# Weight sums of the second MLP product: formed by VectorE beside the product, or by accumulating DMAs in DRAM during the scan

## The chip, the cores and the metric

The kernel runs on one core of a Trainium2 chip. The metric is device time in microseconds for one execution of the whole program, taken as the median of several executions. Beside it stands one profiled execution, whose trace gives every instruction on TensorE (PE, with its weight loads as PEld), VectorE (DVE), ScalarE (ACT), GpSimd (POOL) and SyncE (SP), and every DMA. The clock that TensorE was granted in that execution was 0.999 of full speed.

## The reference

One decoder layer over 16 meta tokens and 512 tokens of width 1024. The front half projects the normed input, mixes tokens by causal pooling and by a Mamba-2 scan in chunks of 128 tokens (8 groups of 4 heads), gates the two branches and multiplies by `w_o`. The back half is a squared-ReLU MLP:

```python
v = rmsnorm(h, mlp_norm_w[i])
hid = jax.nn.relu(v @ w_ff1[i])
h = h + (hid * hid) @ w_ff2[i]      # 512x4096 by 4096x1024
out = rmsnorm(h, final_norm_w)[:, N_META:]
```

All is float32. What the change touches is the last product, `(hid * hid) @ w_ff2`.

## The kernel before, in words

**Precision and operands.** Every large product is made of three TensorE passes on a high and a low part of each operand. A weight block of 128x1024 (512 KB) is loaded by SyncE, its high part is a ScalarE copy and its low part a VectorE subtraction of the high part from the block. In the front half this is `block()` (lines 78 to 93): three tiles for the raw block (`raw`), four pairs for the parts (`whi`, `wlo`). In the back half the same is done by `split` (lines 924 to 930).

**The scan.** Lines 706 to 714 run over eight groups, g = 0 to 7. Each turn weaves the steps of `ssd(g)` (line 448), the scan of group g, with the steps of a projection for the next group, so that TensorE always has matmuls between the scan's small ones. `ssd(g)` begins with one DMA from GpSimd's queue (line 456): it broadcasts the cumulated decays of the group from DRAM to a 1 MB tile `abc`. There is one such tile, so the load waits until the matmuls `py` of the group before (line 543) have read it. ScalarE then makes `eb` from it (line 491), ScalarE and VectorE turn it into the decay matrix (lines 494 to 503), VectorE masks it (line 530), and the `py` matmuls read it (line 543). The instructions of each engine are issued in one fixed order.

In groups 1, 2, 3 and 5 (`SUMS_AT`) the weave has a third member, `sums_of_u` (line 682): it loads two blocks of the projected input from DRAM by GpSimd's queue, forms sums of them on VectorE, and stores high and low parts into the DRAM tiles `t_d` (lines 702 and 703). After the scan, 16 GpSimd DMAs load these again (lines 831 to 833) for the pooling products, which begin with `pool_pair` (line 758). Later, GpSimd's queue loads the residual `ht` (line 964). Nothing else uses GpSimd's queue; it is served in order.

**The MLP.** The hidden width of 4096 is cut into eight pieces c of 512. For each piece four tiles of the first product (`ff1_tile`, line 1122) give the squared activations. The second product of pieces 0 to 6 is made by a scheme with seven products of half-size blocks in place of eight: activations are cut into two token halves and two hidden halves, the weights of a piece into four quarters of 512 KB called b11, b12, b22 and b21. The scheme needs the activation sums S1 to S4 (made in `ff1_tile`) and four weight sums:

- t1 = b11 + b12
- t2 = t1 + b22
- s3 = b12 + b22
- t4 = t2 + b21

In the kernel before, `quarter` (line 1115) loads the four quarters by SyncE into a pool of six tiles, and `sum_of` (line 1175) makes the four sums on VectorE, three of them in place. The loop is at lines 1213 to 1240. Each of the seven operands (b11, t2, s3, t4, b22, b21, t1) is split, and its `prod` (line 1157) is 12 matmuls with 512 columns. Between the products stand `ff1_tile` calls (`filler`). Piece 7 is done without the scheme (lines 1244 to 1276), and each token tile is normed and stored as it is finished. On the host, `_weight_blocks` packs all weights into one input `w`, in the order in which SyncE loads them.

Of the kernel before, what the change touches and what calls it, by code (L numbers as in the profile page):

```python
# [57 lines left out]
def kernel(ctx: ExitStack, tc, xT, x, w, vec, fnw, out):  # L58
    nc = tc.nc
    act, dve, pe, pool = nc.scalar, nc.vector, nc.tensor, nc.gpsimd  # L60

# [620 lines left out]
    def sums_of_u(k, g):  # L682
        a, b = (tsp.tile([P, 2 * TN], F32, tag=t, name=f"{t}{k}") for t in ("ua", "ub"))

        with tc.issue_after(abc_load[g].ins):
            for t, kk in ((a, k), (b, k + 4)):
                nc.gpsimd.dma_start(t, u_d[kk])
        yield
        with tc.issue_after(masked[g].ins):
            dve.tensor_tensor(a[:, one], a[:, two], a[:, one], op=ALU.subtract)  # L690
            dve.tensor_tensor(a[:, two], b[:, two], a[:, two], op=ALU.subtract)
            dve.tensor_tensor(b[:, two], b[:, two], a[:, one], op=ALU.subtract)
            dve.tensor_tensor(b[:, one], b[:, one], b[:, two], op=ALU.subtract)
        yield
        for src, n in ((a, "13"), (b, "42")):
            hi, lo = (tsp.tile([P, 2 * TN], F32R, tag=f"t{p}", name=f"t{p}{n}{k}") for p in "hl")
            if n == "42":
                yield
            with tc.issue_after((y_first if n == "13" else squared)[g].ins):
                act.copy(hi, src)  # L700
            dve.tensor_tensor(lo, src, hi.bitcast(F32), op=ALU.subtract)
            nc.gpsimd.dma_start(t_d[n, "h", k], hi)
            nc.gpsimd.dma_start(t_d[n, "l", k], lo)
# [220 lines left out]
    def split(src):  # L924
        hi = wp.tile([P, 1024], F32R, tag="whi", name=f"shi{nsplit[0]}")
        lo = wp.tile([P, 1024], F32R, tag="wlo", name=f"slo{nsplit[0]}")
        nsplit[0] += 1
        act.copy(hi, src)  # L928
        dve.tensor_tensor(lo, src, hi.bitcast(F32), op=ALU.subtract)  # L929
        return hi, lo  # L930
# [181 lines left out]
    NC = 8  # L1112
    rel = {}

    def quarter(tag):
        b = nblk[0]
        nblk[0] += 1
        t = qp.tile([P, 1024], F32, tag="quarter", name=f"{tag}{b}")
        nc.sync.dma_start(t, w[b])
        return t  # L1120

    def ff1_tile(c, f):
# [49 lines left out]
    p2v = [p2[:, :512], p2[:, 512:]]  # L1172
    q5v = [psum1(f"q5_{t}") for t in range(2)]

    def sum_of(a, b, name, out=None):
        t = out if out is not None else qp.tile([P, 1024], F32, tag="quarter", name=name)
        dve.tensor_tensor(t, a, b, op=ADD)
        return t

    def squares(t, c, n):  # L1180
        act.activation(junk[:, : c.stop - c.start], ht[:, t, c], AF.Square, accum_out=fs[:, t, n : n + 1])

# [28 lines left out]
            ff1_tile(*order.pop(0))  # L1211

    for c in range(NC - 1):
        b11, b12, b22, b21 = (quarter(n) for n in ("b11_", "b12_", "b22_", "b21_"))
        z, e = c == 0, c == NC - 2
        prod(av, c, A11, split(b11), True, False)
        onto(0, 0, alpha, ADD)
        t1 = sum_of(b11, b12, "", b11)
        t2 = sum_of(t1, b22, f"t2_{c}")
        filler()  # L1220
        prod(av, c, S2, split(t2), False, False)
        onto(0, 1, alpha, SUB)
        filler()
        prod(av, c, S3, split(sum_of(b12, b22, "", b12)), False, False)
        onto(1, 1, alpha, SUB)
        filler()
        prod(av, c, A22, split(sum_of(t2, b21, "", t2)), False, True)
        onto(1, 0, alpha, ADD)
        if e:
            prod(q5v, c, S1, split(t1), z, True)  # L1230
# [5 lines left out]
        prod(av, c, S4, split(b22), True, True)  # L1236
        onto(0, 1, alpha, ADD)
        prod(p2v, c, A12, split(b21), z, False)
        if not e:
            prod(q5v, c, S1, split(t1), z, False)  # L1240
    assert not order


# [1 line left out]
    hh, hl = rel[c]  # L1245
    wq = {}
    for k, half in ((1, 0), (1, 1), (0, 1), (0, 0)):
        wq[k, half] = split(quarter(f"w{k}{half}_"))
    lastp = psum2("last")
    for t in range(4):  # L1250
        T, st = t // 2, slice((t % 2) * P, (t % 2 + 1) * P)
# [28 lines left out]
def _weight_blocks(i):  # L1280

    w_in, w_g, w_up = i["w_in"][0], i["pool_w_group"][0], i["w_pool_up"][0]
    w_so, w_o, f1, f2 = i["w_ssd_out"][0], i["w_o"][0], i["w_ff1"][0], i["w_ff2"][0]
    blocks = []

    def cols(m, c):
        a = m[:, c : c + P]
        return a.reshape(NK, P, P).transpose(1, 0, 2).reshape(P, NK * P)

    def put(b):  # L1290
        blocks.append(b)
# [68 lines left out]
    def quarters(c):  # L1360
        for k, half in ((1, 0), (1, 1), (0, 1), (0, 0)):
            put(quarter(c, k, half))
# [9 lines left out]
    for c in range(8):  # L1372
        quarters(c)
        for _ in range(3 if c > 4 else 4):
            ff1()
    return np.ascontiguousarray(np.stack(blocks))


def _vectors(i):
# [35 lines left out]
```

## Time and profile before

| | |
|---|---|
| Time, median of 3 | 1012.66 us (1012.47 to 1012.91) |
| The profiled execution's own time | 1013.65 us |
| Its span, first to last instruction | 1012.0 us |
| DMA traffic | 118.41 MB, mean 117 GB/s |
| GpSimd's DMA queue (q0) | 23.86 MB, 6.8% of the time of 16 DMA engines |
| SyncE's DMA queue (q1) | 92.75 MB, 28.3% |

The profile gives, for each engine, busy time and its share of the span. A view by stretches of time gives the same for each stretch, with the mean busy share of the 16 DMA engines and the bytes per second. The timeline lists instructions in order: start, duration, engine, line, operation, operands, and in square brackets how long the engine stood idle before it and what ended that. The list of DMA issues gives the size of each and the median time from its issue to the landing of its last byte. The time that lies outside the span, 1013.65 - 1012.0 = 1.65 us, has no instruction.

### The profile page before, as it was taken

Reading aid. Unit: us, or ns where it says so; the run is one execution under the profiler, and the core shown is the slowest. Engines: PE = TensorE matmul, PEld = TensorE weight load, DVE = VectorE, ACT = ScalarE, POOL = GpSimd, SP = SyncE. Lnnn points to the kernel's source line nnn. Section 1 sums busy time; section 2 is a strip of 40 time slices with the busy share of each in tenths; the row PEclk is TensorE's granted clock in tenths of the full one; section 3 lists DMA queues with packets and bytes.
Section 4 is the critical chain, followed back from the end, with each engine's and each line's share of the span. In section 5 each row is a group of like instructions: output and inputs, shape, how many; then the busy total and the mean of one; then the engine's idle time right before and its main releaser. Section 6 shows DMA issues by size and latency. Waiting matters only on the chain.

```text
span 1012.0 us, 14216 instructions
## 1 busy us (share of the span) xinstructions
PE 1002.7 (99%) x5661; PEld 866.4 (86%) x5661; DVE 763.4 (75%) x1039; ACT 561.9 (56%) x748; POOL 35.8 (4%) x72
## 2 busy tenths in 40 slices
PE   9999999999999999999999999999999999999997
PEld 7889899998889998978898888888888888888886
DVE  7988798978736587888789557887676686676866
ACT  8665958595827439473355333466545455354444
POOL 0010000101000000003000001000000000000000
PEclk9999999999999999999999999999999999999999
DMA  7263243616224231418334534033333324323112
GB/s 245 84 237 114 67 137 115 204 50 201 66 91 147 101 126 43 146 39 258 102 104 162 193 104 171 17 138 113 104 104 104 105 83 125 104 84 125 42 42 83
DMA packets 35602, 118.41 MB, mean 117 GB/s; under 512 B 4112, under 2 KB 5456, under 8 KB 34512
## 3 DMA queue, kind: packets, MB, share of 16 engines
q1 hardware_dynamic: 26928, 92.75, 28.3%
q0 software_dynamic: 7888, 23.86, 6.8%
q8 instruction: 44, 0.72, 0.3%
q10 hardware_dynamic: 720, 0.91, 0.2%
q14 instruction: 22, 0.18, 0.1%
HBM read 108.94 MB, written 8.55 MB: 116 GB/s over the span
## 4 chain that ended last, share of the span: by engine, by line
PE 96%; DVE 2%; DMA 1%; ACT 0%; issue 0%; SPq 0%; ACTq 0%
PE px L183 11%; PE alpha L1165 6%; PE pf L120 6%; PE pf L122 6%; PE pf L119 6%; PE px L185 6%; PE pz L183 5%; PE alpha L1168 3%; PE pgp L183 3%; PE pgs L183 3%; PE pz L185 3%; PE py L543 2%; PE pso L119 2%; PE po L537 1%; PE pso L120 1%; PE pgp L185 1%
## 5 line engine op out<-in xcount | busy, mean ns | idle before, releaser
L87 ACT CAST whi<-raw 128x1024 fp32r<-128x1024 f32 (+2 forms) x122 | 124.1, 1024 | 168.8 <-PE pf L120 47.0
L88 DVE TENSOR_TENSOR wlo<-raw,whi 128x1024 fp32r<-128x1024 f32 (+2 forms) x122 | 144.2, 1186 | 92.6 <-ACT whi L87 64.4
L183 PE MATMUL px<-uh,whi 128*128 128x264 f32 (+1 forms) x448 | 113.2, 291 | 0.0
L185 PE MATMUL px<-ul,whi 128*128 128x264 f32 (+1 forms) x448 | 110.5, 285 | 0.0
L119 PE MATMUL pf<-vh,whi 128*128 128x512 f32 x256 | 99.9, 390 | 0.0
L120 PE MATMUL pf<-vl,whi 128*128 128x512 f32 x256 | 99.8, 390 | 0.0
L183 PEld LDWEIGHTS px<-uh,whi 128*128 128x128 f32 x448 | 84.7, 189 | 1.8 <-issue 1.4
L185 PEld LDWEIGHTS px<-ul,whi 128*128 128x128 f32 x448 | 84.4, 188 | 0.4 <-issue 0.2
L929 DVE TENSOR_TENSOR slo<-b,shi 128x1024 fp32r<-128x1024 f32 x35 | 42.8, 1221 | 28.8 <-ACT shi L928 15.2
L122 PE MATMUL pf<-vh,wlo 128*128 128x512 f32 x256 | 63.6, 390 | 0.0
L928 ACT CAST shi<-b 128x1024 fp32r<-128x1024 f32 x35 | 36.8, 1051 | 44.8 <-PE pf L120 30.2
L183 PE MATMUL px<-uh,wlo 128*128 128x264 f32 (+1 forms) x448 | 58.5, 283 | 0.0
L122 PEld LDWEIGHTS pf<-vh,wlo 128*128 128x128 f32 x256 | 48.1, 188 | 10.0
L119 PEld LDWEIGHTS pf<-vh,whi 128*128 128x128 f32 x256 | 48.1, 188 | 9.9
L120 PEld LDWEIGHTS pf<-vl,whi 128*128 128x128 f32 x256 | 48.1, 188 | 9.8
L183 PEld LDWEIGHTS px<-uh,wlo 128*128 128x128 f32 x448 | 55.9, 189 | 0.0
L1165 PE MATMUL alpha<-shi,hh 128*128 128x512 f32 x140 | 54.6, 390 | 0.0
L1168 PE MATMUL alpha<-shi,hl 128*128 128x512 f32 x140 | 54.5, 390 | 0.0
L995 DVE TENSOR_TENSOR ht<-ht,alpha 128x1024 f32<-128x1024 f32 x35 | 42.6, 1218 | 15.7 <-PE alpha L1165 15.7
L183 PE MATMUL pz<-uh,whi 128*128 128x512 f32 x112 | 43.7, 391 | 0.1
L185 PE MATMUL pz<-ul,whi 128*128 128x512 f32 x112 | 43.7, 390 | 0.0
L564 DVE RECIPROCAL rs<-rs 128x128 f32<-128x128 f32 x32 | 27.2, 909 | 13.7 <-ACT rs L562 13.6
(503 smaller groups left out, 2422.0 us busy)
## 6 DMA issues: line engine op xcount, KB each, us to landing
raw<-in_w SPq DMA_DIRECT2D x128, 512.0 KB, 3.6
b<-in_w SPq DMA_DIRECT2D x28, 512.0 KB, 3.6
abc<-acs_d POOLq DMA_DIRECT2D x8, 1024.0 KB, 6.8
wob<-in_w SPq DMA_DIRECT2D x8, 512.0 KB, 5.9
xt<-in_xT SPq DMA_DIRECT2D x8, 264.0 KB, 5.5
u_d<-xt POOLq DMA_DIRECT2D x8, 260.0 KB, 2.8
ht<-in_x POOLq DMA_DIRECT2D x4, 512.0 KB, 5.5
w<-in_w SPq DMA_DIRECT2D x4, 512.0 KB, 3.5
```

The costliest lines, as they stand in the source:

```text
L87: act.copy(hi[:, c], raw[:, c])
L88: dve.tensor_tensor(lo[:, c], raw[:, c], hi[:, c].bitcast(F32), op=ALU.subtract)
L119: pe.matmul(ps, ah, bh, start=first and n == 0, stop=False)
L120: pe.matmul(ps, ah, bl, start=False, stop=False)
L122: pe.matmul(ps, al, bh, start=False, stop=last and n == len(pairs) - 1)
L183: pe.matmul(o, wt, rhs[0][k][:, c], start=part == 0 and k == 0, stop=part == 1 and k == NK - 1)
L185: pe.matmul(o, wt, rhs[1][k][:, c], start=False, stop=False)
L928: act.copy(hi, src)
L929: dve.tensor_tensor(lo, src, hi.bitcast(F32), op=ALU.subtract)
L995: dve.tensor_tensor(o, o, src, op=op)
L1165: pe.matmul(ps[t], hh[:, p, seg, st], m, start=bool(first and not low and p == 0), stop=bool(last and low and p == 1), skip_group_check=True)
L1168: pe.matmul(ps[t], hl[:, p, seg, st], m, start=False, stop=False, skip_group_check=True)
```

## The change

The 28 quarters of pieces 0 to 6 leave `w` and become an input of their own, `f2`, of shape 7 x 4 x 128 x 1024. `w` keeps the first product's blocks and piece 7's quarters in the order of use.

For each piece, four DRAM tiles (rows of 1024 values at a pitch of 1040) receive t1, t2, s3 and t4. They are made by DMAs alone, issued from GpSimd's queue: a plain DMA copies the first addend from `f2` (or from a finished sum) into the tile, and a DMA with `accum_op=add` adds a quarter onto it. That is eight DMAs of 512 KB for each piece, four copies and four additions, 56 in all. Where one reads what another wrote, it waits for it.

They are a further member of the weave: piece 0 in group 0, pieces 1 and 2 in group 4, pieces 3 and 4 in group 6, pieces 5 and 6 in group 7. They stand behind the `abc` load of their group in GpSimd's queue.

In the MLP all seven operands of a piece are loaded by SyncE, each where its product is, three from `f2` and four from the DRAM sums: 49 loads for pieces 0 to 6 in place of 28. The 28 additions on VectorE are gone.

```diff
+SUMS2_AT = {0: (0,), 4: (1, 2), 6: (3, 4), 7: (5, 6)}
...
+    SUMS = ("t1", "t2", "s3", "t4")
+    f2s = {(n, c): dram.tile([P, 1040], F32, name=f"f2{n}_{c}")[:, :1024] for n in SUMS for c in range(f2.shape[0])}
+
+    def sums_of_f2(cs, g):
+        B11, B12, B22, B21 = range(4)
+
+        def copy(n, src):
+            for c in cs:
+                nc.gpsimd.dma_start(f2s[n, c], f2[c, src] if isinstance(src, int) else f2s[src, c])
+
+        def add(n, src):
+            for c in cs:
+                nc.gpsimd.dma_start(f2s[n, c], f2[c, src], accum_op=ALU.add)
+
+        with tc.issue_after(abc_load[g].ins):
+            copy("t1", B11)
+            copy("s3", B12)
+            add("t1", B12)
+            add("s3", B22)
+            copy("t2", "t1")
+            add("t2", B22)
+            copy("t4", "t2")
+            add("t4", B21)
+        yield
...
+        if g in SUMS2_AT:
+            fill.append(sums_of_f2(SUMS2_AT[g], g))
...
     for c in range(NC - 1):
-        b11, b12, b22, b21 = (quarter(n) for n in ("b11_", "b12_", "b22_", "b21_"))
         z, e = c == 0, c == NC - 2
-        prod(av, c, A11, split(b11), True, False)
+
+        def weights(n):
+            direct = {"b11": 0, "b22": 2, "b21": 3}
+            return split(quarter(f"{n}_{c}", f2[c, direct[n]] if n in direct else f2s[n, c]))
+
+        prod(av, c, A11, weights("b11"), True, False)
         onto(0, 0, alpha, ADD)
-        t1 = sum_of(b11, b12, "", b11)
-        t2 = sum_of(t1, b22, f"t2_{c}")
         filler()
-        prod(av, c, S2, split(t2), False, False)
+        prod(av, c, S2, weights("t2"), False, False)
...
-        prod(av, c, S3, split(sum_of(b12, b22, "", b12)), False, False)
+        prod(av, c, S3, weights("s3"), False, False)
...
-        prod(av, c, A22, split(sum_of(t2, b21, "", t2)), False, True)
+        prod(av, c, A22, weights("t4"), False, True)
```

The products t1, b22 and b21 change in the same way. In the order of GpSimd's queue after the change, group 6 reads: the `abc` load of group 6; copies of t1 for pieces 3 and 4; copy of s3 for piece 3; the store of `t_d42h` (line 702 before); copy of s3 for piece 4; addition to t1 of piece 3; the store of `t_d42l` (line 703 before); additions to t1 of piece 4, s3 of 3, s3 of 4; copies of t2 for 3 and 4; additions to t2 for 3 and 4; copies of t4 for 3 and 4; additions to t4 for 3 and 4; the `abc` load of group 7. In group 4 the stores of `t_d` stand likewise among the first copies, ahead of the first addition. In groups 0 and 7 nothing stands between them. The instructions of the other engines keep their order but for a handful of neighbours that change places (one cast of `sums_of_u` on ScalarE, one matmul of `pso`, one small product on VectorE, the split of ScalarE's decay steps into runs).

More of the change, by code (lines that the diff above doesn't have):

```diff
@@ L57, with kernel @@
 @with_exitstack
-def kernel(ctx: ExitStack, tc, xT, x, w, vec, fnw, out):
+def kernel(ctx: ExitStack, tc, xT, x, w, f2, vec, fnw, out):
     nc = tc.nc
@@ L1113, with quarter @@
     rel = {}
[L1115 to L1119, printed above, removed]
+    def quarter(name, src):
+        t = qp.tile([P, 1024], F32, tag="quarter", name=name)
+        nc.sync.dma_start(t, src)
         return t
@@ L1173 @@
     q5v = [psum1(f"q5_{t}") for t in range(2)]
[L1175 to L1178, printed above, removed]
     def squares(t, c, n):
@@ L1213 @@
     for c in range(NC - 1):
-        b11, b12, b22, b21 = (quarter(n) for n in ("b11_", "b12_", "b22_", "b21_"))
         z, e = c == 0, c == NC - 2
-        prod(av, c, A11, split(b11), True, False)
+        def weights(n):
+            direct = {"b11": 0, "b22": 2, "b21": 3}
+            return split(quarter(f"{n}_{c}", f2[c, direct[n]] if n in direct else f2s[n, c]))
+        prod(av, c, A11, weights("b11"), True, False)
         onto(0, 0, alpha, ADD)
-        t1 = sum_of(b11, b12, "", b11)
-        t2 = sum_of(t1, b22, f"t2_{c}")
         filler()
-        prod(av, c, S2, split(t2), False, False)
+        prod(av, c, S2, weights("t2"), False, False)
         onto(0, 1, alpha, SUB)
         filler()
-        prod(av, c, S3, split(sum_of(b12, b22, "", b12)), False, False)
+        prod(av, c, S3, weights("s3"), False, False)
         onto(1, 1, alpha, SUB)
         filler()
-        prod(av, c, A22, split(sum_of(t2, b21, "", t2)), False, True)
+        prod(av, c, A22, weights("t4"), False, True)
         onto(1, 0, alpha, ADD)
         if e:
-            prod(q5v, c, S1, split(t1), z, True)
+            prod(q5v, c, S1, weights("t1"), z, True)
             for t in range(2):
@@ L1235 @@
             filler()
-        prod(av, c, S4, split(b22), True, True)
+        prod(av, c, S4, weights("b22"), True, True)
         onto(0, 1, alpha, ADD)
-        prod(p2v, c, A12, split(b21), z, False)
+        prod(p2v, c, A12, weights("b21"), z, False)
         if not e:
-            prod(q5v, c, S1, split(t1), z, False)
+            prod(q5v, c, S1, weights("t1"), z, False)
     assert not order
@@ L1247 @@
     for k, half in ((1, 0), (1, 1), (0, 1), (0, 0)):
-        wq[k, half] = split(quarter(f"w{k}{half}_"))
+        b = nblk[0]
+        nblk[0] += 1
+        wq[k, half] = split(quarter(f"w{k}{half}_{b}", w[b]))
     lastp = psum2("last")
@@ L1358, in quarter @@
         return np.concatenate(a, 1)
-    def quarters(c):
-        for k, half in ((1, 0), (1, 1), (0, 1), (0, 0)):
-            put(quarter(c, k, half))
+    quarters = [[quarter(c, k, half) for k, half in ((1, 0), (1, 1), (0, 1), (0, 0))] for c in range(8)]
     ff = list(range(32))
@@ L1371, in _weight_blocks @@
         ff1()
[L1372 to L1376, printed above, removed]
+    while ff:
+        ff1()
+    blocks += quarters[7]
+    return np.ascontiguousarray(np.stack(blocks)), np.ascontiguousarray(np.array(quarters[:7]))
 def _vectors(i):
@@ L1402 @@
         "in_x": np.ascontiguousarray(x),
-        "in_w": _weight_blocks(i),
+        "in_w": blocks,
+        "in_f2": f2,
         "in_vec": _vectors(i),
```

1 line of the change is left out of this document (added).

## The prediction

> **What bounds the kernel now.** I read the page's busy times and its chain first, then the view by stretches of time.
>
> ```profile
> span 1012.0 us, 14216 instructions
> ...
> PE 1002.7 (99%) x5661; PEld 866.4 (86%) x5661; DVE 763.4 (75%) x1039; ACT 561.9 (56%) x748; POOL 35.8 (4%) x72
> ...
> PE 96%; DVE 2%; DMA 1%; ACT 0%; issue 0%; SPq 0%; ACTq 0%
> ```
>
> ```profile
> core 0: us, PE busy (x) PEld busy (x) DVE busy (x) ACT busy (x) POOL busy (x), PEclk, DMA share, GB/s
> 0.00:25.00 25.00, 22.67 (x183) 19.44 (x184) 18.16 (x37) 20.38 (x34) 0.94 (x7) 1.00 0.75 245
> 25.00:225.00 200.00, 199.82 (x1357) 180.62 (x1356) 168.92 (x278) 143.31 (x196) 16.18 (x30) 1.00 0.38 128
> 225.00:250.00 25.00, 24.88 (x192) 22.76 (x191) 22.88 (x36) 13.67 (x17) 2.51 (x5) 1.00 0.54 180
> 250.00:425.00 175.00, 175.00 (x1153) 156.11 (x1152) 119.67 (x181) 101.01 (x137) 5.03 (x10) 1.00 0.31 103
> 425.00:450.00 25.00, 24.10 (x127) 19.68 (x127) 19.01 (x33) 23.45 (x32) 0.00 (x0) 1.00 0.16 54
> 450.00:690.00 240.00, 240.00 (x1260) 205.73 (x1256) 184.88 (x259) 105.33 (x154) 11.17 (x21) 1.00 0.42 139
> 690.00:985.00 295.00, 295.00 (x1303) 244.35 (x1302) 212.76 (x187) 143.77 (x154) 0.00 (x0) 1.00 0.30 93
> 985.00:1012.00 27.00, 21.21 (x105) 17.66 (x103) 17.16 (x34) 11.02 (x27) 0.00 (x0) 0.95 0.20 78
> ```
>
> TensorE is the bound everywhere. Of its 9.3 us without work, 2.3 lie in the first 25 us and 5.8 in the last 27. Between them are 1.2 us, 0.90 of which stand at 425 to 450, in the last group of the scan. In the MLP (690 to 985) it is busy for 295.00 of 295 us at full clock. So nothing taken from another engine there can shorten the run, and anything that makes TensorE wait is added in full, because it has no idle time in which to catch up.
>
> **What is removed: 28 additions on VectorE.**
>
> ```profile
> L1177 DVE TENSOR_TENSOR b<-b,b x14: 1217/1222/1227, 694.3 to 950.1; 128x1024 f32<-128x1024 f32 x14
> L1177 DVE TENSOR_TENSOR t<-b,b x7: 1225/1226/1226, 695.6 to 944.3; 128x1024 f32<-128x1024 f32 x7
> L1177 DVE TENSOR_TENSOR t<-t,b x7: 1220/1221/1224, 705.2 to 951.3; 128x1024 f32<-128x1024 f32 x7
> L928 ACT CAST shi<-b 128x1024 fp32r<-128x1024 f32 x35 | 36.8, 1051 | 44.8 <-PE pf L120 30.2 <-PE alpha L1168 12.1 <-DVE b L1177 2.5
> L1119 SPq DMA_DIRECT2D b<-in_w x28: 327/328/432, 671.8 to 931.0; - x28
> DMA to landing us min/median/max: 3.3/3.6/5.6
> ```
>
> 14 x 1.222 + 7 x 1.226 + 7 x 1.221 = 34.2 us of VectorE's 212.8 in that stretch. TensorE covers them today: ScalarE's cast, the step before the product, waited 44.8 us, of which 42.3 for TensorE to give operand tiles back and 2.5 for a sum. Value: 0.
>
> **What is added in the MLP: 21 loads.** 49 in place of 28, 21 x 512 KB = 11.0 MB over 295 us, or 37 GB/s on top of 93; the share of the DMA engines goes from 0.30 to some 0.42. A load lands 3.6 us after its issue; six tiles serve as buffers, so a load is issued when the operand six before it has been split, some six products of 12 matmuls ahead. The four sums that are loaded were finished hundreds of microseconds before. Value: 0. If that cover were gone, a late block would cost about one landing, 3.6 us.
>
> **What is added in the scan: 56 DMAs on GpSimd's queue.** Each takes GpSimd about 0.54 us to issue (rows below), 30 us of an engine that is 4% busy. The price lies in their waits. GpSimd serves its queue in order, and a DMA that reads a sum still in flight makes it stand. Behind it stand the `abc` loads of groups 1, 5 and 7 and the 16 loads of `t_d`. The timeline of GpSimd has the times at which these go out now:
>
> ```profile
> 63.60 0.55 POOL L456 DMA_DIRECT2D abc<-acs_d  x1
> 96.01 0.55 POOL L456 DMA_DIRECT2D abc<-acs_d  x1 [31.86 <-PE py L543]
> ...
> 302.25 0.54 POOL L456 DMA_DIRECT2D abc<-acs_d  x1 [52.09 <-DVE wlo L88]
> ...
> 374.11 0.54 POOL L456 DMA_DIRECT2D abc<-acs_d  x1 [1.66 <-PE py L543]
> 380.75 0.53 POOL L702 DMA_DIRECT2D t_d42h<-th  x1 [6.11 <-ACT th L700]
> 384.71 0.53 POOL L703 DMA_DIRECT2D t_d42l<-tl  x1 [3.42 <-DVE tl L701]
> 418.36 0.55 POOL L456 DMA_DIRECT2D abc<-acs_d  x1 [33.12 <-DVE xc L396]
> 455.43 2.13 POOL L833 DMA_DIRECT2D t13h<-t_d13h  x4 [36.52 <-PE py L543]
> ```
>
> The room is 32 us for piece 0's eight DMAs (64 to 96), 52 us for sixteen in group 4, 44 us in group 6 (374 to 418, but the first addition comes behind a store that goes out at 380.75), and 36 us in group 7.
>
> What a DRAM-to-DRAM copy or addition costs, no row shows. The nearest rows are stores to DRAM, loads by GpSimd's queue, and the rate over 40 slices of 620 to 640 us, where several loads of 512 KB are under way:
>
> ```profile
> u_d<-xt POOLq DMA_DIRECT2D x8, 260.0 KB, 2.8
> DMA to landing us min/median/max: 3.9/5.5/7.6
> GB/s 0 180 197 336 401 361 385 229 8 0 66 90 328 393 418 442 434 410 393 434 434 426 410 393 393 434 377 16 0 0 0 0 0 0 0 0 0 0 0 0
> ```
>
> At 434 GB/s one pass of 512 KB (524,288 bytes) takes 1.2 us and 260 KB 0.6 us, so the fixed part of a store is 2.8 - 0.6 = 2.2 us. The second line is of the four `ht` loads, issued 0.54 us apart: each lands later than the one before, so what is queued is worked off one behind the other.
>
> A **copy** lies between one pass, 1.2 us (reading beside writing), and two, 2.4 us. I take 2.4, the dearer end, since both sides are DRAM here and SyncE's weight loads share the engines. An **addition** reads two operands and writes one. Its low end is 2.4 us (two reads, the write beside them); three passes make 3.6, twice a copy 4.8, and its high end is twice three passes, 7.2 us, an adder at half the stream's rate. The traffic row lies nearest to 3.6 to 4.8; I take the middle, 4.2.
>
> [...]
>
> **Group 6 worked out** with a = 4.2:
> - The four copies are through at 386.2: the last is issued at 381.3 behind the store of 380.75, its neighbours ahead of it in the queue.
> - The four additions to t1 and s3 follow one behind the other: 4 x 4.2 = 16.8, with a store of 0.6 among them, to 403.6.
> - The first copy of t2 lands 2.4 + 0.9 later, 406.9 (of the fixed 2.2 us I put 1.3 ahead of the transfer and 0.9 behind).
> - Two additions to t2: 1.3 + 8.4 + 0.9, to 417.6. The last copy of t4: 4.6 and a little, to 422.4.
> - The last addition goes out at 422.4, the `abc` load of group 7 at 423.0 instead of 418.36. Two additions are ahead of it in the queue (421.6 + 8.4 = 430.0), then its 1 MB: 2.4 + 0.9. It lands at 433.2.
>
> Eight additions lie in that chain, so it moves by 8 us for each 1 us of a: 428.4 at 3.6, 438.0 at 4.8, 447.6 at 6.0, 457.2 at 7.2.
>
> When must it be there? In order: the landing of that load today (from its issue), then ScalarE, VectorE and TensorE in the last group:
>
> ```profile
> DMA to landing us min/median/max: 7.1/7.1/7.1
> 428.30 1.06 ACT L491 ACTIVATE eb<-abc 64x1024 f32<-64x1024 f32 x1
> ...
> 443.53 1.06 ACT L502 ACTIVATE abc<-abc 128x1024 f32<-128x1024 f32 x1
> 446.99 2.29 DVE L530 TENSOR_TENSOR abc<-abc,cbm 128x2048 f32<-128x2048 f32 x1
> 449.39 1.09 PE L543 MATMUL py<-abc,xdt 128*64 128x128 f32 x16 [0.90 <-PE psp L663]
> ```
>
> It lands at 418.36 + 7.1 = 425.5 and is read at 428.30: 2.8 us of room. From there ScalarE is busy for 23.45 of 25 us, VectorE masks at 446.99, and TensorE already waits 0.90 us for that at 449.39. Behind the waiting read in ScalarE's order stand the SiLU of the last group, its root and its casts; all are late with it. So what exceeds 428.3 goes to TensorE one for one: 433.2 - 428.3 = **4.9 us**.
>
> **The other chains**, by the same steps: piece 0's ends in time, its `abc` load at 96.01 as before, landing at 101.8 with the queue. Group 4's last addition is out at about 287, ahead of 302.25. Group 7's delays the sixteen loads only to a last landing at 483.5, and their first reading is late:
>
> ```profile
> 107.76 1.06 ACT L491 ACTIVATE eb<-abc 64x1024 f32<-64x1024 f32 x1
> L787 PE MATMUL pxx<-t42h,whiS x12: 279/282/286, 511.8 to 540.9; 128*128 128x260 f32 x12
> ```
>
> 6 us of room for group 1, 28 for the loads. Value 0 each. The stores of `t_d` that stand behind copies, and one behind an addition issued at 381.8, go out when their data is ready, as now: 0. Neighbours that change places on ScalarE, VectorE and TensorE: 0, the same work.
>
> **Sum.** 0 + 0 + 4.9 on the profiled execution's 1013.65 gives 1018.55. The median of the runs stands 0.99 below that execution, so 1017.6.
>
> **Rivals.**
> - *Not slower: the additions keep pace.* At 3.6 us (three passes) or less, the load of group 7 lands by 428.4, and the waits hide in GpSimd's idle time; 1012.7. It decides at a = 3.6 with copies at 2.4; for it speaks that GpSimd is 96% idle and the DMA engines are 0.31 busy there, against it the eight additions in a row.
> - *A slow adder*, a = 7.2: 28.9 us at group 7, and piece 0's chain lands group 1's load at 113.8 against 107.76, 6.0 more: 1013.65 + 34.9 - 0.99 = 1047.6. No row speaks for or against it.
> - *VectorE's relief pays*: at most the 1.2 us that TensorE idles between 25 and 985, 1011.5, which is within 0.2%; 0.90 of it belongs to the scan, which is not relieved. More would have to come out of the first 25 or the last 27 us, where the change touches nothing.
> - *The sums are loaded late in the MLP*, or the new traffic delays weights: one block, 3.6 us, 1016.3; against it speaks the lead of six operands.
>
> **How the numbers follow.** Forecast case (late by 2 to 20 us, a from about 3.85 to 6.1) 0.43, own range 1014.7 to 1033; additions in pace 0.39; slow adder 0.12; late loads 0.03; faster 0.03. A measurement of this kernel can tell about 0.2%, 2 us, from no change. Slower: 0.43 + 0.12 + 0.03 = 0.58, within 0.2% 0.39, faster 0.03. The range takes the case without loss (0.5 us below the median) to the slow adder: 1012.2 to 1047.6.
>
> **What would show it.** Right: in group 6 the `abc` load goes out after 418.4 behind an addition, ScalarE's `eb` of the last group stands idle for that DMA, TensorE's idle time at 425 to 450 grows from 0.9 to some 6 us, and 690 to 985 stays full. The list of DMA issues gives copy and addition their landing times: some 4.6 and 6.4 us alone. Wrong: that load out on time; or TensorE idle at other groups, at the pooling products or in the MLP; or VectorE's time in the MLP not 34 us down.

## The result and the profile after

The changed kernel takes **1018.75 us** (median of 6 runs, 1015.65 to 1023.3) against 1012.59 us (6 runs, 1012.3 to 1012.91): 1.0062 times as long, 95% interval 1.0035 to 1.009. Not only the median has moved: the runs of the kernel before lie within 0.6 us, those of the changed one spread over 7.65. The profiled execution is the slowest of the six, 1023.3 us. Its page, the lines that answer to those shown of before:

```profile
span 1021.1 us, 14309 instructions
...
PE 1006.8 (99%) x5661; PEld 868.6 (85%) x5661; DVE 732.0 (72%) x1011; ACT 561.4 (55%) x748; POOL 74.5 (7%) x128
...
PE 92%; ACT 3%; DVE 2%; DMA 2%; issue 1%; POOL 0%; ACTq 0%; POOLq 0%
```

The span is 9.1 us longer. TensorE's time without work grows from 1012.0 - 1002.7 = 9.3 to 1021.1 - 1006.8 = 14.3, by 5.0 us. The other 4.1 us are in its busy time: the same 5661 matmuls took longer, at a granted clock of 0.995 in place of 0.999. In the same stretches as before:

```profile
25.00:225.00 200.00, 199.82 (x1356) 180.52 (x1356) 169.03 (x279) 143.14 (x196) 21.72 (x38) 1.00 0.47 149
225.00:250.00 25.00, 25.00 (x192) 23.09 (x191) 21.32 (x33) 11.76 (x15) 4.27 (x8) 1.00 0.71 233
250.00:425.00 175.00, 173.11 (x1130) 153.73 (x1129) 118.63 (x179) 101.64 (x137) 27.50 (x42) 0.99 0.64 178
425.00:450.00 25.00, 20.76 (x102) 16.98 (x101) 12.47 (x24) 16.14 (x24) 4.40 (x6) 0.93 1.00 278
450.00:690.00 240.00, 239.38 (x1262) 204.79 (x1261) 188.50 (x265) 108.78 (x158) 15.68 (x27) 1.00 0.48 151
690.00:985.00 295.00, 295.00 (x1302) 244.10 (x1301) 177.53 (x158) 143.91 (x158) 0.00 (x0) 1.00 0.44 138
```

The MLP (690 to 985) has lost VectorE's sums, 212.76 down to 177.53 us, and TensorE fills all 295 us as it did before. The losses are two, both in the scan: 1.9 us at 250 to 425, and at 425 to 450, where the DMA engines are now busy for the whole time (1.00 in place of 0.16).

**The loss in the last group.** GpSimd's timeline around the `abc` load of group 7, and under it the landing time of that load:

```profile
414.05 0.53 POOL L718 DMA_DIRECT2D f2t<-f2t  x1 [2.12 <-DMA f2t<-in_f]
419.01 1.69 POOL L722 DMA_DIRECT2D f2t<-in_f  x2 [4.43 <-DMA f2t<-f2t]
421.47 0.59 POOL L458 DMA_DIRECT2D abc<-acs_d  x1 [0.77 <-issue]
```

```profile
DMA to landing us min/median/max: 14.5/14.5/14.5
```

The load goes out at 421.47, 3.1 us after the 418.36 of before, and by then the whole execution is 3 us late from group 4. It was the `py` matmuls that held it back, as before, and not the additions: group 6's last ones end at 417.80 before and at 420.90 after, and each time the load goes out some 0.6 us later. So its issue is not late. Its landing is: 14.5 us after the issue in place of 7.1, behind the two additions of 419.01. Next ScalarE's and TensorE's timelines of the changed kernel:

```profile
436.07 1.28 ACT L493 ACT_TABLE_LOAD   x1 [5.98 <-DMA abc<-acs_d]
437.36 1.06 ACT L493 ACTIVATE eb<-abc 64x1024 f32<-64x1024 f32 x1
```

```profile
440.43 0.28 PE L472 MATMUL ptm<-ident,xc 128*16 128x128 f32 x1 [1.60 <-ACT xc L400]
444.02 0.65 PE L480 MATMUL ptx<-ident,xc 128*128 128x128 f32 x4 [2.64 <-DVE xdtm L473]
458.39 1.09 PE L545 MATMUL py<-abc,xdt 128*64 128x128 f32 x16 [0.62 <-PE psp L665]
```

ScalarE stands 5.98 us for the load, and TensorE then stands 1.60 + 2.64 + 0.62 = 4.86 us where it stood 0.90.

**The loss in group 4**, which the prediction had priced at 0. ScalarE's cast of the second half of the pooling sums, first in the kernel before, then in the changed one, and under them the changed kernel's GpSimd and TensorE:

```profile
246.19 0.63 ACT L700 CAST th<-ub 128x520 fp32r<-128x520 f32 x1 [2.02 <-DMA t_d13h<-th]
```

```profile
248.52 0.63 ACT L702 CAST th<-ub 128x520 fp32r<-128x520 f32 x1 [2.42 <-DMA t_d13h<-th]
```

```profile
237.37 1.05 POOL L718 DMA_DIRECT2D f2t<-in_f  x2
242.54 0.56 POOL L704 DMA_DIRECT2D t_d13h<-th  x1 [4.12 <-ACT th L702]
```

```profile
265.30 0.50 PE L121 MATMUL pso<-yh,whi 128*128 128x512 f32 x1 [1.66 <-ACT yh L573]
266.02 0.51 PE L122 MATMUL pso<-yl,whi 128*128 128x512 f32 x1 [0.23 <-DVE yl L574]
```

The store of `t_d13h` goes out at 242.54, when its data is ready, but two copies of 512 KB were issued at 237.37. The cast that reuses its tile waits until 248.52, 6.0 us after the store's issue (3.4 before). From there ScalarE is busy without a break and hands `yh` over 1.66 us late.

**The lower clock.** Stretches of 4 us of the changed kernel, with TensorE's busy time as the second number and the granted clock third from the end:

```profile
264.00:268.00 4.00, 2.48 (x7) 1.63 (x8) 3.54 (x8) 4.00 (x9) 0.00 (x0) 0.89 0.95 315
268.00:272.00 4.00, 4.00 (x17) 2.97 (x15) 2.01 (x4) 3.87 (x5) 1.65 (x2) 0.68 0.56 99
...
440.00:444.00 4.00, 0.95 (x6) 0.64 (x6) 1.22 (x6) 3.93 (x6) 2.42 (x3) 1.00 1.04 164
444.00:448.00 4.00, 3.98 (x13) 3.19 (x14) 2.63 (x5) 3.96 (x5) 0.54 (x1) 0.58 1.03 176
```

After these two waits the clock falls, to 0.68 and 0.58 in a stretch of 4 us. Worked out from these rows, an estimate, that is 4 x (0.11 + 0.32 + 0.42) = 3.4 of the 4.1 us. In this execution, then, the lower clock behind the waits was a second price, beside 5.0 us of idle time.

### The profile page after: what moved, and what is told of

Same layout as the page of the kernel before. It is cut to its first block, busy times and chain, and to the rows that moved or that the text cites. A ratio compares the mean times of both kernels' runs of the same rounds, so it can differ in the third digit from the quotient of the medians.

```text
span 1021.1 us, 14309 instructions
## 1 busy us (share of the span) xinstructions
PE 1006.8 (99%) x5661; PEld 868.6 (85%) x5661; DVE 732.0 (72%) x1011; ACT 561.4 (55%) x748; POOL 74.5 (7%) x128
## 4 chain that ended last, share of the span: by engine, by line
PE 92%; ACT 3%; DVE 2%; DMA 2%; issue 1%; POOL 0%; ACTq 0%; POOLq 0%
PE px L185 10%; PE alpha L1195 6%; PE pf L122 6%; PE pf L121 6%; PE pf L124 6%; PE px L187 5%; PE pz L185 4%; PE alpha L1198 3%; PE pgs L185 3%; PE pgp L185 3%; PE pz L187 2%; PE py L545 2%; PE pso L124 2%; PE po L539 1%; PE wo_alpha L1014 1%; DMA abc<-acs_d 1%
## 5 line engine op out<-in xcount | busy, mean ns | idle before, releaser
L961 DVE TENSOR_TENSOR slo<-b,shi 128x1024 fp32r<-128x1024 f32 x21 | 25.7, 1224 | 25.6 <-ACT shi L960 21.5
L1195 PE MATMUL alpha<-slo,hh 128*128 128x512 f32 x140 | 37.4, 389 | 0.0
```

The lines of the kernel that those rows point to most:

```text
L1195: pe.matmul(ps[t], hh[:, p, seg, st], m, start=bool(first and not low and p == 0), stop=bool(last and low and p == 1), skip_group_check=True)
```

## The experiments

After the result three theories stood. **A**, queue order: what stands behind copies and additions in GpSimd's queue is late. **B**, traffic: 56 transfers of 512 KB fill the DMA engines and delay whatever else uses them. **C**, the MLP's new loads. Two more came later, both forms of B: **D**, the traffic delays weight blocks wherever it is put, and **E**, it does so only where the weight loads have little lead, that is few buffers. All twelve runs, against the kernel before on the same chip:

| run | median us (range, runs) | ratio, 95% interval |
|---|---|---|
| mlp_loads_alone | 1013.15 (1012.35 to 1013.5, 10) | 1.0003 [0.9994, 1.0013] |
| scan_dmas_alone | 1016.52 (1015.08 to 1019.86, 5) | 1.0042 [1.0025, 1.0058] |
| last_adds_behind_load | 1017.24 (1016.12 to 1018.22, 4) | 1.0044 [1.0029, 1.0059] |
| copies_behind_stores | 1015.8 (1014.08 to 1016.76, 5) | 1.0029 [1.0016, 1.0042] |
| both_repairs | 1015.66 (1014.42 to 1016.97, 8) | 1.0029 [1.0019, 1.0039] |
| copies_for_additions | 1015.1 (1013.23 to 1016.81, 9) | 1.0022 [1.0012, 1.0032] |
| sums_after_scan | 1031.7 (1029.85 to 1032.19, 5) | 1.0184 [1.017, 1.0198] |
| group_6_alone | 1013.7 (1012.79 to 1018.99, 11) | 1.0016 [1.0005, 1.0027] |
| sums_in_mlp | 1014.57 (1013.33 to 1018.55, 12) | 1.0022 [1.0014, 1.003] |
| group_7_alone | 1012.98 (1012.46 to 1014.08, 11) | 1.0004 [0.9995, 1.0013] |
| no_pair_at_group_7 | 1015.93 (1013.38 to 1021.52, 8) | 1.0037 [1.0021, 1.0053] |
| group_4_alone | 1016.62 (1014.89 to 1017.52, 5) | 1.0036 [1.0022, 1.0049] |

### The MLP part alone, the scan part alone

In mlp_loads_alone no sums are formed and the loads take quarters as they are; in scan_dmas_alone the 56 DMAs run as in the change and the MLP is that of the kernel before. The first as a diff against the changed kernel:

```diff
-SUMS2_AT = {0: (0,), 4: (1, 2), 6: (3, 4), 7: (5, 6)}
+SUMS2_AT = {}
...
-            direct = {"b11": 0, "b22": 2, "b21": 3}
-            return split(quarter(f"{n}_{c}", f2[c, direct[n]] if n in direct else f2s[n, c]))
+            src = {"b11": 0, "b22": 2, "b21": 3, "t1": 0, "t2": 1, "s3": 1, "t4": 2}
+            return split(quarter(f"{n}_{c}", f2[c, src[n]]))
```

> No sums are formed: the 56 DMAs of the scan are left out, and each of the 49 loads in the MLP takes a quarter as it is (t1 takes b11, t2 and s3 take b12, t4 takes b22), so the output is not that of the MLP. Theory A (the loss is made in the scan, by what stands ahead of urgent DMAs in GpSimd's queue): 1012.6 us, within 0.5, TensorE without an idle row between 25 and 1000 us but the 0.9 of before. Theory B (the loss is made by DMA traffic beside other work, wherever it is): 1012.6 to 1014. Theory C (part of the loss lies in the 21 added loads of the MLP): 1014 or more, TensorE under 295 of 295 us in the MLP.

> The kernel before with the 56 DMAs of the scan added and their results unused; the MLP forms its sums on VectorE as before. Theories A and B: all of the loss, 1015.5 to 1023 with a median near 1018.7, with ScalarE waiting some 6 us for the decay load of the last group and TensorE idle some 4 us at 425 to 450. Theory C: less than half of the loss, under 1015.5.

Stretches of the first and then of the second, TensorE's busy time behind the length:

```profile
240.00:290.00 50.00, 50.00 (x253) 41.40 (x253) 33.15 (x51) 34.10 (x45) 2.13 (x4) 1.00 0.34 111
420.00:470.00 50.00, 49.13 (x265) 40.79 (x264) 42.16 (x65) 31.40 (x40) 3.73 (x7) 1.00 0.45 138
690.00:985.00 295.00, 295.00 (x1302) 244.07 (x1301) 182.65 (x161) 143.39 (x154) 0.00 (x0) 1.00 0.39 126
```

```profile
240.00:290.00 50.00, 48.43 (x245) 39.54 (x245) 31.29 (x49) 34.09 (x45) 12.15 (x18) 1.00 0.98 270
420.00:470.00 50.00, 47.30 (x264) 39.20 (x263) 39.74 (x62) 31.61 (x41) 14.06 (x23) 1.00 0.96 265
```

The MLP part does nothing that can be measured: 30 us less on VectorE and 21 loads more leave TensorE at 295.00 of 295. Theory C falls, and with it the hope of a gain. The scan part alone costs 3.8 us by the medians (interval 2.5 to 5.9), at the two places where the changed kernel lost; ScalarE's wait for the last `abc` load is 2.5 us in its profile, not the 6 that were expected. The remaining 2.2 us to the changed kernel's median can't be told from nothing: the two intervals overlap.

### Two repairs of the queue's order

In last_adds_behind_load group 6's last two additions go behind the `abc` load of group 7:

```diff
+            if g == 7:
+                for c in SUMS2_AT[6]:
+                    nc.gpsimd.dma_start(f2s["t4", c], f2[c, B21], accum_op=ALU.add)
...
-            add("t4", B21)
+            if g != 6:
+                add("t4", B21)
```

In copies_behind_stores group 4's sixteen DMAs go behind the last store of group 3's sums (`stored` holds the stores); both_repairs has the two edits together:

```diff
-        with tc.issue_after(abc_load[g].ins):
+        if g == 4:
+            while (2, "42") not in stored:
+                yield
+        with tc.issue_after((stored[2, "42"] if g == 4 else abc_load[g]).ins):
```

> The changed kernel with group 6's last two additions issued behind the decay load of group 7 in place of ahead of it; every byte is moved as before. Theory A: that load lands about 7 us after its issue instead of 14.5, the idle time of TensorE in the last group falls from 4.2 us to about 1, and only the loss of group 4 stays: 1014.5 to 1017. Theory B: the two additions go on beside the load, it lands after 11 us or more, and the time stays near 1018.7.

> The changed kernel with group 4's sixteen DMAs issued behind the last store of the projected sums (t_d) of that group in place of among and ahead of those stores; every byte is moved as before. Theory A: the stores land after about 2.7 us as in the kernel before, ScalarE's cast no longer waits longer for them, TensorE idles nowhere at 250 to 275, group 5 begins at 302.3 instead of 306.0, and only the loss of the last group stays: 1015 to 1019, some 3 to 4 us under the changed kernel beside it. Theory B: the traffic falls into the same stretch of time, and the time stays near 1018.7.

> The changed kernel with both edits at once: group 4's sixteen DMAs go behind the last store of t_d of that group, and group 6's last two additions go behind the load of abc for the last group. Theory A (the loss is the order in GpSimd's queue): both loads and stores are as early as in the kernel before, TensorE is busy 50.00 of 50 us at 240 to 290 and at least 49 of 50 at 420 to 470; time within 1 us of the kernel before, 1012.7 to 1013.7. Theory B (the loss is the bytes that pass through the shared DMA engines, whoever stands first): the group-4 wait goes, but at 420 to 470 TensorE still loses 2 us or more, now behind late weight blocks; 1015 to 1017.

In the first, the load lands 8.1 us after its issue, as A said (B had 11 us or more), and no instruction waits for it. Yet the time, 1017.24, is hardly better, and just above the 1017 that A allowed. ScalarE's and then TensorE's timeline of that run show what took its place:

```profile
455.21 1.05 ACT L635 CAST whi<-raw 128x1024 fp32r<-128x1024 f32 x1 [4.22 <-DMA raw<-in_w]
462.04 1.04 ACT L89 CAST whi<-raw 128x1024 fp32r<-128x1024 f32 x1 [3.14 <-DMA raw<-in_w]
```

```profile
463.65 0.50 PE L561 MATMUL png<-qhg,ones_r 128*128 128x512 f32 x1 [1.56 <-ACT qhg L297]
```

The weight blocks at 420 to 470 land there in a median of 7.4 us (6.3 in the changed kernel, 4.3 before), and what ScalarE has queued behind the waiting cast is late with it. In these profiles TensorE loses 2.47 us at 420 to 470 where the changed kernel lost 4.86, and another 0.90 at 470 to 500. So a wait was in part moved and not removed; that fits B.

The same profile, of a run of 1016.12, shows something about group 4, whose order this edit leaves as it was. ScalarE's cast there, and the stretch:

```profile
245.76 0.63 ACT L702 CAST th<-ub 128x520 fp32r<-128x520 f32 x1
240.00:290.00 50.00, 50.00 (x254) 41.30 (x254) 33.37 (x51) 34.05 (x45) 12.16 (x18) 1.00 0.97 274
```

The cast found its tile free, and TensorE lost nothing. The two copies ahead of the store of `t_d13h` landed in 6.7 and 7.4 us, where the changed kernel's took 9.1 and 9.9, and the store in 3.5 in place of 6.0. In the profiles of scan_dmas_alone, copies_for_additions and group_4_alone the copies took 8.6 to 9.6 and the store 5.6 to 6.0, and the wait was there. So group 4's wait is in some executions and not in others, by how long the copies ahead of the store take. That is one way in which runs of one kernel can differ.

In copies_behind_stores group 4 is whole again, and the load of group 7 is late as in the changed kernel:

```profile
240.00:290.00 50.00, 50.00 (x251) 40.80 (x251) 32.80 (x51) 33.92 (x45) 12.97 (x20) 1.00 0.91 257
420.00:470.00 50.00, 46.15 (x251) 37.94 (x250) 38.66 (x60) 30.75 (x40) 13.07 (x20) 1.00 1.00 267
```

Its median lies 2.95 us below the changed kernel's, which fits group 4's part (3.8 us alone, below), though the two intervals overlap. A's forecast of 1015 to 1019 held, B's did not. The edit takes the copies' place in the queue and their traffic away from the stores together, so it doesn't tell the two apart. Both repairs together gain nothing over this one. In that profile TensorE is whole at 240 to 290 and lacks 1.35 us at 420 to 470 and 0.84 behind it, but the median stays 3.0 us above the kernel before. A's forecast of 1012.7 to 1013.7 missed. B's time of 1015 to 1017 held, but not its 2 us or more at 420 to 470.

### Plain copies in place of the additions

```diff
-                nc.gpsimd.dma_start(f2s[n, c], f2[c, src], accum_op=ALU.add)
+                nc.gpsimd.dma_start(f2s[n, c], f2[c, src])
```

> The changed kernel with each of the 28 additions replaced by a plain copy of the same block (what is loaded is then not the weight sums): same order, same waits, the same count of DMAs on GpSimd's queue, only without the second operand's read and the addition. Theory A with the addition's size as in the prediction (an addition's transfer is more than a copy's, eight of them in group 6's chain): the chain shortens by eight times some 1.8 us, 14 us, so the load of abc for the last group is issued no later than in the kernel before, has nothing long ahead of it and lands within 9 us; TensorE at 420 to 470 loses 1 us or less, time 1013 to 1014.5. Theory B: additions cost what their bytes cost, and two thirds of the bytes remain; the loss shrinks but stays, 1014.5 to 1016.5.

The chain of group 6 shortens: its last member goes out at 411.41 instead of 419.01, 8.2 us ahead of the load. The load lands in 7.3 us, and TensorE has 49.09 of 50 us at 420 to 470, as in the kernel before. What is left stands in group 4 (48.46 of 50 at 240 to 290), where the stores stand behind first copies and not behind additions. The time, 1015.1, lies in B's forecast (1014.5 to 1016.5) and above A's (1013 to 1014.5), though the load and TensorE at 420 to 470 did what A said; A's sum had left group 4 out.

What a single DMA costs is read where one runs all but alone, in group 0 of the changed kernel. Its GpSimd timeline there, and then the landing times of all its additions and of all its copies:

```profile
83.03 0.54 POOL L718 DMA_DIRECT2D f2t<-f2t  x1 [5.53 <-DMA f2t<-in_f]
86.83 0.81 POOL L722 DMA_DIRECT2D f2t<-in_f  x1 [3.26 <-DMA f2t<-f2t]
```

```profile
DMA to landing us min/median/max: 5.3/8.3/12.8
```

```profile
DMA to landing us min/median/max: 3.5/8.8/18.4
```

The copy of 83.03 and the addition of 86.83, with little else under way (an addition that lands at 85.0 beside the copy, a weight block issued at 90.9 beside the addition), are the two shortest, 3.5 and 5.3 us. In company an addition takes 8.3 in the median and up to 12.8, a copy up to 18.4.

### One group at a time

```diff
-SUMS2_AT = {0: (0,), 4: (1, 2), 6: (3, 4), 7: (5, 6)}
+SUMS2_AT = {6: (3, 4)}
```

This is group_6_alone; the others have `{7: (5, 6)}` and `{4: (1, 2)}`, and in all three the MLP loads the quarters as they are for the pieces without sums.

> Only pieces 3 and 4 have their sums formed, in group 6; groups 0, 4 and 7 have no DMA of the change, and the MLP loads the other pieces' quarters as they are in place of the sums (same loads, the output is not the MLP's). The prediction's step priced this chain alone at the whole loss, 4.9 us. If that is so: the load of abc for the last group lands 12 us or more after its issue, TensorE loses 4 to 6 us at 420 to 470, time 1016 to 1018. If group 4's stores and group 7's traffic carry the rest: 1 to 3 us at 420 to 470 and 50.00 of 50 at 240 to 290, 1014 to 1015.5.

> Only pieces 5 and 6 have their sums formed, in group 7 (the other pieces' quarters are loaded as they are in place of the sums, the output is not the MLP's). No DMA of the change stands ahead of the load of abc of the last group; sixteen stand behind it, beside eight weight loads with three buffers. Theory A (queue order alone): nothing of the scan is behind them but the sixteen loads of t_d, which have 28 us of room; no loss, 1012.7. Theory E (traffic delays weight blocks with little lead): blocks land in 7 us in place of 4.3 at 420 to 470, TensorE loses 1 to 2.5 us between 420 and 480; 1013.7 to 1015.2. Together with the 1.0 us of group 6 alone and the group-4 part this should make up the loss of the whole scan part, 3.8 us.

> Only pieces 1 and 2 have their sums formed, in group 4, with the stores of t_d of group 3's sums between the copies as in the changed kernel (the other pieces' quarters are loaded as they are in place of the sums, the output is not the MLP's). Theory A (those stores stand in the queue behind copies, ScalarE's cast and VectorE's subtraction wait for the tiles to come free, pso waits for yh): TensorE loses 1.5 to 2 us at 260 to 267 and some more by the lower clock behind it, nothing at 420 to 470; with group 6 alone at 1.0 and group 7 alone at 0.3 us, some 2.5 us are left for it of the scan part's 3.8: 1014.5 to 1015.5. If group 4 matters only in company of the others: 1012.7 to 1013.3, TensorE 50.00 of 50 at 240 to 290, and the losses of the groups don't add.

**Group 6** costs 1.0 us by the medians, not the 4.9 of the prediction. In its profile (1012.79 us) the last two additions lie 7.8 and 4.1 us ahead of the load, not both within 2.5 us, and the load lands in 7.8 us. GpSimd's timeline:

```profile
410.20 0.82 POOL L722 DMA_DIRECT2D f2t<-in_f  x1 [1.22 <-DMA f2t<-f2t]
413.88 0.82 POOL L722 DMA_DIRECT2D f2t<-in_f  x1 [2.85 <-DMA f2t<-f2t]
417.96 0.60 POOL L458 DMA_DIRECT2D abc<-acs_d  x1 [3.25 <-issue]
```

Nine of its eleven runs lie between 1012.79 and 1014.65, two at 1017.23 and 1018.99. The chain ends within a few microseconds of the load; whether those two runs are ones in which it ended later was not profiled. Their granted clock is 0.997 and 0.996, that of the nine others 0.998 to 1.000; against 0.999 that is some 2 and 3 us, an estimate, of the 3.5 and 5.3 by which they lie above the median.

**Group 7** alone costs nothing that can be measured (1.0004), though weight blocks at 420 to 470 land there in a median of 7.3 us. What its traffic adds when late additions of group 6 are ahead of it was not run apart.

**Group 4** alone costs 3.8 us, more than the 1.0 and 0.3 of the other two together, and by the wait seen in the changed kernel. TensorE's timeline and stretches of that run:

```profile
265.50 0.50 PE L121 MATMUL pso<-yh,whi 128*128 128x512 f32 x1 [1.68 <-ACT yh L573]
```

```profile
264.00:268.00 4.00, 2.28 (x8) 1.47 (x9) 3.54 (x7) 4.00 (x9) 0.15 (x1) 1.00 1.01 304
268.00:272.00 4.00, 4.00 (x23) 3.21 (x21) 2.71 (x6) 3.97 (x5) 1.67 (x2) 1.00 0.47 147
```

The expectation put 1014.5 to 1015.5; the median is 1016.62. In the profile (1015.58) the clock stayed at 1.00 behind the same wait that had brought 0.89 and 0.68 in the changed kernel. That the slower runs of this kernel are those in which it falls, the clocks of the runs don't bear out: 0.999 in the profiled run and 0.998 in the four others, the fastest (1014.89) among them. The three groups alone add to 5.1 us. The scan part's 3.8 has an interval of 2.5 to 5.9 and the changed kernel's 6.1 one of 3.5 to 9.1, so the sum fits both.

### The sums elsewhere

In sums_after_scan piece 0 stays in group 0, and behind the sixteen loads of `t_d` stands:

```diff
+    for cs in (1, 2), (3, 4), (5, 6):
+        for _ in sums_of_f2(cs, None, t_load):
+            pass
```

In sums_in_mlp the same three lines stand behind the load of `fw`. In no_pair_at_group_7 the table is `{0: (0,), 4: (1,), 6: (2,)}`, group 4's DMAs behind the stores, and the pairs (3, 4) and (5, 6) behind the load of `fw`.

> Only piece 0's sums are formed in the scan; those of pieces 1 to 6 are issued on GpSimd's queue behind the sixteen loads of t_d, from about 486 us, in three pairs, where that queue has nothing else to do until about 624 and TensorE waits for nothing. The same 56 DMAs, the same loads in the MLP. Theories A and B: what costs time is that the traffic meets the short waits of groups 4, 6 and 7 of the scan; the sums are done by about 620, the first is read at about 720, TensorE is 49 of 50 busy at 420 to 470 and 240 of 240 at 450 to 690, time 1012.5 to 1013.5. Theory D (the traffic delays weight blocks wherever it is put): TensorE loses 2 us or more between 486 and 620, 1015 or more. No theory expects a gain over the kernel before, since TensorE stays the bound.

> The same 48 DMAs of pieces 1 to 6 as in the run with the sums behind the scan (1031.7 us), put still later: on GpSimd's queue behind the load of fw, from about 636 us, in three pairs, so that they run until about 780. Theory D (the DMAs fill the engines and weight blocks land late whatever the place): TensorE loses as it did there, 10 us or more between 640 and 790; 1022 or more. Theory E (they cost only where the weight loads have little lead: three buffers and a block every 6 us behind the scan, against the MLP with six buffers and a block every 6 to 9 us): the sums of piece 1 are done by about 685, each sum ahead of its load, TensorE stays 295.00 of 295 busy at 690 to 985; 1012.5 to 1014. If a sum is not done when SyncE comes to load it, all weight loads stand behind that load: that would show as SyncE waiting for an addition, and TensorE idle by 3 us or more at each.

> Piece 0 in group 0, piece 1 alone in group 4 behind the stores of t_d, piece 2 alone in group 6, pieces 3 to 6 as two pairs behind the load of fw. One chain at a time in the scan, half the DMAs under way, none in group 7. Theory E: the load of abc for the last group is issued and lands as in the kernel before (7 to 8 us), weight blocks land within 5 us, TensorE loses nothing anywhere that the kernel before doesn't; 1012.5 to 1013.3. Theory D: a loss of 1 us or more at 365 to 420 or behind 640; 1014 or more. VectorE's 34 us less give no theory a gain, as TensorE stays the bound.

**Behind the scan** I expected no loss; it is the dearest place of all, 19 us. The view by stretches, the landing of weight blocks at 470 to 620, and the waits of ScalarE and of TensorE in that time:

```profile
470.00:690.00 220.00, 209.94 (x1071) 178.55 (x1070) 153.24 (x211) 88.41 (x131) 40.04 (x62) 0.98 0.76 228
```

```profile
DMA to landing us min/median/max: 3.5/8.3/16.6
```

```profile
ACT whi L89 <- DMA raw<-in_w: 25.4, 7, 5.2
```

```profile
PE pxx L819 <- DVE pu L833: 2.6, 1, 2.6
PE pup L121 <- ACT yph L851: 1.9, 1, 1.9
PE psl L121 <- DVE acc L875: 1.7, 1, 1.7
```

Here no store and no `abc` load stands behind the chain in GpSimd's queue. SyncE's weight blocks do the suffering: 26 of them in 147 us, one every 5.6, through three buffers, landing in 8.3 us where the kernel before has 3.7. That is B with nothing of A in it, the form D. Of the added time in this profile 10.1 us are waits of TensorE at 470 to 690, and 6.1 us are longer busy time, 1008.8 against 1002.7, at a granted clock of 0.994: the second price again.

**In the MLP**, where the weights have six buffers, the same 48 DMAs cost 1.9 us. TensorE is at 220.00 of 220 and 295.00 of 295 in the profile, although the last weight blocks at 640 to 690 land in a median of 12.5 us. So E (lead decides, not the share of the engines alone) is far nearer than D, whose bound was 1022; but its own bound of 1014 was missed by 0.6, and where those 1.9 us lie the profile (of a run of 1013.33) doesn't show. **One chain at a time** in groups 4 and 6 missed too, 1015.93 against 1013.3 at most. Its profile, of a run of 1014.36, lacks 0.51 us at 680 to 690, where the DMA engines are full (a share of 1.05); D's time of 1014 or more held, without the loss of 1 us or more that it named. No placement tried beat the kernel before, and none could be expected to: TensorE is busy for 99% of the span before and after.

## Why the prediction was right and where it was wrong

Forecast 1017.6, measured 1018.75: right in sign, size and range. That the size came so near is in good part luck: behind it stand one step that was too dear and one that was missing. Two of the prediction's own signs of being wrong came true as well: the load of group 7 went out on time, counted from its group, and TensorE stood idle in group 4.

- **VectorE's sums at 0: right.** 212.76 to 177.53 us, TensorE still full, and 1.0003 with the MLP part alone.
- **The 21 loads at 0: right.** They land in 3.5 to 3.7 us, and with six buffers TensorE stays at 295.00 of 295 us.
- **The prices.** Taking off the same fixed 2.2 us (an estimate: the 2.8 us of a 260 KB store less 0.6 at 434 GB/s), a copy's transfer is an estimate of 1.3 us (I took 2.4) and an addition's 3.1 (4.2); the difference of 1.8 was exact. An addition's transfer is thus 3.1 / 1.3 = 2.4 times a copy's, an estimate from two DMAs that ran all but alone. By the prediction's own threshold of 3.6 the additions should then have kept pace, and the load landed by 428.4. It did not: the prediction assumed DMAs that are worked off one behind the other at the price of a lone one, while two chains and the weight loads share engines that are 0.64 busy over 250 to 425 and 1.00 at the end, and a lone 5.3 us becomes 8.3 in the median.
- **"The `abc` load of group 7 at 423.0 instead of 418.36": wrong.** The last additions went out at 419.01 and did not hold the load back, which went out 0.6 us behind the end of the `py` matmuls, as before. It landed at 436.0, or 432.9 on the clock of before (3.1 us off), against 433.2 predicted. That agreement is two errors that cancel: the load went out 4.6 us earlier than forecast, as its chain was some 6 us faster, and its landing behind two additions took 14.5 us and not 10.2.
- **"Goes to TensorE one for one", 4.9 us:** in this execution 4.86 - 0.90 = 4.0, by the chain the prediction named (ScalarE's `eb`, then `xc`, then the last group). As the price of group 6's chain it is too large: alone, 1.0 us (0.5 to 2.7).
- **"The stores of `t_d` that stand behind copies go out when their data is ready, as now: 0": wrong, and the largest term**, 3.8 us (2.2 to 5.0) with group 4 alone. The first store did go out when ready, but landed 6.0 us after its issue in place of 3.3, and the cast that needed its tile was late with it. It was not so in each execution: in the profile of last_adds_behind_load the store landed in 3.5 us and nothing waited. The step counted the issue and not the landing, and did not ask who waits for the tile that a store holds.
- **Group 7's chain at 0: right**, 1.0004 alone.
- **The clock had no term.** In the profiled execution 4.1 of the 9.1 us are slower matmuls, most of them behind TensorE's waits. That is the slowest of the six runs and the only one at 0.995; the five others are at 0.998 to 1.000.
- **The rivals.** "The additions keep pace" had the lone price on its side and still lost. That "the new traffic delays weights" was right as a mechanism and wrong in place: in the scan it takes over when the queue's order is mended, and behind the scan it costs 19 us.

Open: why the runs of most versions with chains in the scan spread so far. Group 4's wait, which comes or stays away, is one source; a lower clock is another in some of the slowest runs (0.995 at 1023.3 in the changed kernel, 0.996 at 1021.52 in no_pair_at_group_7), but not at 1020.05 and 1020.97, which have 0.998. Open too is what the last 2 to 3 us are in both_repairs and no_pair_at_group_7, whose profiles show less.

## What to carry to other kernels

Free queues and idle engines did not make the transfers free: in the kernel before GpSimd was busy for 4% of the span and the DMA engines for 0.31 of 250 to 425, and the scan's 56 DMAs alone cost 3.8 us. So ask of every other load and store that is in flight beside it how long it may take to land, that is how many buffers it has and who waits for the tile, and look for the least lead and not at the mean share of the DMA engines: the same 48 DMAs cost 19 us behind the scan, where the weight loads have three buffers, and 1.9 us in the MLP, where they have six. Price a DMA in the company it will have; here a lone 5.3 us became 8.3 in the median and 12.8 at most. With TensorE busy for 99% of the span, 30 us taken off VectorE in the MLP were worth nothing (1.0003 in mlp_loads_alone); the new waits of TensorE made the changed kernel's profiled span longer by 5.0 us, and a lower clock, most of it behind two of them, by another 4.1.

## What the runs showed of the hardware

- **Behind a short wait TensorE's clock was halved for a few microseconds in one run, and not in another.** In the changed kernel 1.66 + 0.23 us of waiting at 265 are followed by 0.89 and 0.68, 1.60 + 2.64 us up to 444 by 0.58, each in a stretch of 4 us; in stretches of 2 us the clock is 0.50 at 268 to 270 and at 446 to 448. In group_4_alone the same 1.68 us are followed by 1.00. What decides between the two was not shown.
- **An accumulating DMA took GpSimd longer to issue:** in the changed kernel 0.83 to 0.84 us in the median against 0.53 to 0.54 for a copy of the same 512 KB; the prediction had 0.54 for both.
- **A copy from DRAM to DRAM** of 512 KB that ran all but alone, at 83.03 in the changed kernel, landed in 3.5 us; with 2.2 us fixed (2.8 of a store less 0.6, as above) that is some 400 GB/s, an estimate.
